# Decay sums by DMA from DRAM, in place of TensorE matmuls, in a hybrid state-space, attention and expert layer

## The chip, the cores and the metric

The kernel runs on one NeuronCore of a Trainium2 chip. Its engines are TensorE (PE, with its weight loads as PEld), VectorE (DVE), ScalarE (ACT), GpSimd (POOL) and SyncE (SP); SP, ACT and POOL issue DMAs. The metric is the device time of one execution in microseconds (us). L365 is line 365 of the kernel before.

## The reference: what is computed

One layer over 512 tokens of width 1024, in float32. After a norm and a projection, two branches run: a state-space branch (SSD) with 32 heads in 4 groups, in 4 chunks of 128 tokens, and windowed attention with 16 heads. They are gated, merged, projected and added to x. Then each token goes through 2 of 64 experts. The part that matters here:

```python
a_cum = jnp.cumsum(dt_c * a.reshape(G, J), axis=2)      # 32 heads, 4 chunks of 128 tokens
seg = a_cum[:, :, :, None] - a_cum[:, :, None, :]
decay = jnp.exp(jnp.where(causal, seg, -jnp.inf))
y_diag = jnp.einsum('bclsgj,bcsgjp->bclgjp', cb[..., None] * decay, xdt)
y_off = jnp.einsum('bclgn,bcgjpn->bclgjp', cm, prev) * jnp.exp(a_cum)[..., None]
```

For each head the kernel thus needs the running sums of all 512 tokens, one row of 512 numbers, on every partition, beside the same sums with the token on the partition.

## The kernel before, in words

The first half works with the channels or the tokens on the 128 partitions. proj() (L185) loads 1 MB of weights on SP's queue into one of two w buffers, splits it into a high part (ACT, L181) and a low part (DVE, every fifth time GpSimd, L182), and multiplies in three passes (L196 to L198) into the PSUM tag mm. The stages that call it (xbc_stage, z_stage, gate_stage, yssd0, yssd1) are written in the order of L639 to L673, with ssd_main(g) for the four groups among them. Behind them come the attention output and the output projection (L676 to L769), the router, and the experts (from L772), whose weights stream through two rings of buffers, ra and rb, on SP's queue; rb lies in memory that the first half gives back.

dt_stage (L210) makes the running sums: acum, with a token of a chunk on each partition and 4 x 32 columns (chunk, head). Four transposes turn a doubled copy of it, so that PSUM holds the 32 head rows twice; aT then holds the rows' high parts on partitions 0 to 31 and what is left on 32 to 63, with zeros below. sel holds two stacked identities.

ssd_main(g) makes the products of its group, and then four pairs of heads. decay(i, u) spreads head h's row over the partitions with one matmul (L365: sel's column h as the stationary operand, aT as the moving one) into the PSUM tag sb, which has two banks. ACT takes the exponential of half of it into E (L368), DVE takes the minimum with acum (L369) into M, and ACT takes four exponentials in M, one for each chunk (L374). heads(i) multiplies M with the masked products cbm, on DVE for u = 0 and on GpSimd for u = 1 (L386), runs the matmuls of the pair (L382, L390), and adds what belongs together (L392 to L395). A pair's decay is written one pair ahead of its heads (L397 to L401). cbm, E, M, btok and xx are v tiles, of which there are 10 buffers (L140); ssd_norm, the attention, the output projection and the router use the same tag.

The program order isn't the order on the engines. The tile framework plans each engine's order when the program is built (L1283), with its own estimate of every instruction's time; PE's matmuls of later stages so stand between those of ssd_main. Each engine then runs its list in order, and so does each DMA queue. The sb banks are used by ssd_norm, the attention's scores and the router as well. GpSimd issues the stores of gtd (L636), the gates, which SP loads again as c (L681, L682); ACT issues the loads of g2t (L702), a row of 512 numbers spread over 128 partitions from DRAM.

Of the kernel before, what the change touches and what calls it, by code (L numbers as in the profile page):

```python
# [7 lines left out]
F = mybir.dt.float32  # L8
R = mybir.dt.float32r
# [3 lines left out]
AF = mybir.ActivationFunctionType  # L13
OP = mybir.AluOpType
# [16 lines left out]
def tile_hybrid(ctx: ExitStack, tc: tile.TileContext, x, pos, cols, rows, g2d, wrd, wdtd, wcm, wqkv, wso, wao, wo,  # L31
                wgu, wdn, out):
    nc = tc.nc
    V, S, T, G = nc.vector, nc.scalar, nc.tensor, nc.gpsimd
# [4 lines left out]
    def ptile(tag, bufs=2, dt=F):  # L39
        return psum.tile([128, 512], dt, name=tag, tag=tag, bufs=bufs)  # L40

    p1 = ctx.enter_context(ExitStack())
    py, pg, pw, px, pb, pc, pz, pv = [p1.enter_context(tc.tile_pool(name=n, bufs=1, side="right"))
                                      for n in ("py", "pg", "pw", "px", "pb", "pc", "pz", "pv")]
# [4 lines left out]
    ident = cp.tile([128, 128], F, name="ident")  # L49
# [15 lines left out]
    mhalf, half = mh2[:, 0:1], mh2[:, 1:2]  # L65
    V.memset(mhalf, -0.5)
    V.memset(half, 0.5)
    sel = pb.tile([128, 32], R, name="sel")
    G.memset(sel.bitcast(F), 0.0)
    V.tensor_tensor(sel[0:64], ident[0:64, 0:32], ident[0:64, 32:64], op=OP.add)  # L70
    colt = pb.tile([128, 168], F, name="colt")
    S.dma_start(colt, cols)
    n1g, sng, dsk, n2g = colt[:, 0:8], colt[:, 8:24], colt[:, 24:40], colt[:, 160:168]
# [40 lines left out]
    dram = ctx.enter_context(tc.tile_pool(name="dram", bufs=1, space=bass.MemoryType.DRAM))  # L114
    h2d = dram.tile([512, 1024], F, name="h2d")
    tabd = dram.tile([128, 4 * NBK], I32, name="tabd")
    gwd = dram.tile([1024, 1], F, name="gwd")
    gtd = dram.tile([2, 8, 128, 512], F, name="gtd")

    def wslot(pool, tag, bufs, dt=F):  # L120
        return pool.tile([128, 2048], dt, name=tag, tag=tag, bufs=bufs)
# [8 lines left out]
    def tk(pool, tag, bufs, n, dt=F, name=None):  # L130
        return pool.tile([128, n], dt, name=name or tag, tag=tag, bufs=bufs)
# [5 lines left out]
    def a_(dt=F): return tk(pa, "a", 8, 512, dt)  # L137
    def w_(): return tk(pw, "w", 2, 2048, F)
    def g_(): return tk(pg, "g", 4, 1024, R)
    def v_(dt=F, n=512): return pv.tile([128, n], dt, name="v", tag="v", bufs=10, padded_shape=[128, 512])  # L140
    def c_(dt=F, n=512): return pc.tile([128, n], dt, name="c", tag="c", bufs=6, padded_shape=[128, 512])


# [2 lines left out]
    for t in range(4):  # L146
        xt = [x_(), x_()]
        for u in range(2):
            nc.sync.dma_start(xt[u], x[t * 128:(t + 1) * 128, u * 512:(u + 1) * 512])
        xs_.append(xt)  # L150
    wdt = v_(n=256)
    nc.sync.dma_start(wdt, wdtd)
    for t in range(4):
# [12 lines left out]
    for k in range(8):  # L166
        p = ptile(("tp", "sb", "y", "tp")[k // 2])
# [34 lines left out]
    dt = pb.tile([128, 128], F, name="dt")  # L202
    acum = pb.tile([128, 128], F, name="acum")
    dec = pb.tile([128, 128], F, name="dec")
    cd = pb.tile([128, 128], F, name="cd")
    nacum = pb.tile([128, 128], F, name="nacum")
    aT = pb.tile([128, 512], R, name="aT")
    G.memset(aT[64:128].bitcast(F), 0.0)

    def dt_stage():  # L210
        wd = g_()
        V.memset(wd.bitcast(F), 0.0)
        w3 = wd.rearrange("p (k c) -> p k c", k=8)
        r3 = wdt.rearrange("p (k c) -> p k c", k=8)
        S.activation(w3[:, :, 0:32], r3, AF.Copy)
        V.tensor_tensor(w3[:, :, 32:64], r3, w3[:, :, 0:32].bitcast(F), op=OP.subtract)
        p = ptile("mm")
        for k in range(8):
            T.matmul(p, w3[:, k, :], hh[k], start=(k == 0), stop=False)
            T.matmul(p, w3[:, k, :], hl[k], start=False, stop=(k == 7))  # L220
        dtT = v_()
        S.activation(dtT[0:64], p[0:64], AF.Copy)
        p = ptile("tp")
        for t in range(4):
            T.transpose(p[:, t * 64:(t + 1) * 64], dtT[0:64, t * 128:(t + 1) * 128], ident[0:64, 0:64])
        p3 = p[:, 0:256].rearrange("p (t u h) -> p t u h", t=4, u=2)
        xr = v_(n=128)
        x3 = xr.rearrange("p (t h) -> p t h", t=4)
        V.tensor_tensor(x3, p3[:, :, 0, :], dtb[:, None, :].to_broadcast([128, 4, 32]), op=OP.add)
        V.tensor_tensor(x3, x3, p3[:, :, 1, :], op=OP.add)  # L230

        e = v_(n=128)
        V.tensor_scalar(e, xr, -1.0, None, op0=OP.mult)
        V.tensor_tensor(e, e, xr, op=OP.min)
        S.activation(e, e, AF.Exp)
        s1 = v_(n=128)
        V.tensor_scalar(s1, e, 2.0, None, op0=OP.add)
        V.reciprocal(s1, s1)
        V.tensor_tensor(s1, s1, e, op=OP.mult)
        s2 = v_(n=128)  # L240
        V.tensor_tensor(s2, s1, s1, op=OP.mult)
        q = v_(n=128)
        V.tensor_scalar(q, s2, 1.0 / 17, 1.0 / 15, op0=OP.mult, op1=OP.add)
        for c in (13, 11, 9, 7, 5, 3, 1):
            V.tensor_tensor(q, q, s2, op=OP.mult)
            V.tensor_scalar(q, q, 1.0 / c, None, op0=OP.add)
        V.tensor_tensor(q, q, s1, op=OP.mult)
        V.tensor_scalar(xr, xr, 0.0, None, op0=OP.max)
        V.scalar_tensor_tensor(dt, q, 2.0, xr, op0=OP.mult, op1=OP.add)
        ea = v_(n=32)  # L250
        S.activation(ea, alog, AF.Exp)
        da = v_(n=128)
        V.scalar_tensor_tensor(da.rearrange("p (t h) -> p t h", t=4), dt.rearrange("p (t h) -> p t h", t=4), -1.0,
                               ea[:, None, :].to_broadcast([128, 4, 32]), op0=OP.mult, op1=OP.mult)
        pc = ptile("tp")
        T.matmul(pc[:, 0:128], tri, da, start=True, stop=True)
        T.matmul(pc[:, 128:256], ones, da, start=True, stop=True)
        V.tensor_copy(acum, pc[:, 0:128])
        V.tensor_scalar(nacum, acum, -1.0, None, op0=OP.mult)
        S.activation(cd, pc[:, 128:256], AF.Exp)  # L260
        V.tensor_tensor(dec, pc[:, 128:256], acum, op=OP.subtract)
        S.activation(dec, dec, AF.Exp)
        a2 = v_(n=256)
        a2v = a2.rearrange("p (t u h) -> p t u h", t=4, u=2)
        for u in range(2):
            V.tensor_copy(a2v[:, :, u, :], acum.rearrange("p (t h) -> p t h", t=4))
        pt = ptile("tp")
        for t in range(4):
            T.transpose(pt[0:64, t * 128:(t + 1) * 128], a2[:, t * 64:(t + 1) * 64], ident)
        S.activation(aT[0:32], pt[0:32], AF.Copy)  # L270
        hv = v_(R)
        S.activation(hv[32:64], pt[32:64], AF.Copy)
        V.tensor_tensor(aT[32:64], pt[32:64], hv[32:64].bitcast(F), op=OP.subtract)

    dt_stage()


# [44 lines left out]
    def ssd_main(g):  # L322
        BT, CT = bc[g, 0], bc[g, 1]
        p = ptile("tp")
# [6 lines left out]
        p = ptile("tp")  # L331
# [10 lines left out]
        for c in range(4):  # L342
            p = ptile("tp")
# [16 lines left out]
        def decay(i, u):  # L360
            h = 8 * g + 2 * i + u
            if u == 0:
                Es[i] = v_()
            pb_ = ptile("sb")
            T.matmul(pb_, sel[:, h:h + 1].to_broadcast([128, 128]), aT, start=True, stop=True)  # L365
            M = v_()
            us = slice(u * 64, (u + 1) * 64)
            S.activation(Es[i][us, 0:384], pb_[us, 128:512], AF.Exp)  # L368
            V.tensor_tensor(M.rearrange("p (c l) -> p c l", c=4), pb_.rearrange("p (c l) -> p c l", c=4),  # L369
                            acum.rearrange("p (c h) -> p c h", c=4)[:, :, h:h + 1].to_broadcast([128, 4, 128]),  # L370
                            op=OP.min)
            for c in range(4):
                s = slice(c * 128, (c + 1) * 128)
                S.activation(M[:, s], M[:, s], AF.Exp, bias=nacum[:, c * 32 + h:c * 32 + h + 1])  # L374
            return M


        def heads(i, Ms):
# [16 lines left out]
            G.tensor_tensor(y[:, 128:512], y[:, 128:512], E[:, 0:384], op=OP.add)  # L395

        both = lambda i: [decay(i, u) for u in range(2)]  # L397
        nxt = both(0)
        for i in range(4):
# [320 lines left out]
    for ct in range(4):  # L720
# [6 lines left out]
        pt = [ptile("tp"), ptile("tp")]  # L727
        for tp in range(2):
            p = ptile("mm")
            for ti in range(2):  # L730
                t = 2 * tp + ti
# [98 lines left out]
    for q in range(3):  # L830
        T.matmul(pk[:, q * 64 + 64:256], oneb, ob[:, None, q * 64:(q + 1) * 64].to_broadcast([128, 3 - q, 64]),
                 start=False, stop=False)
# [3 lines left out]
                    op=OP.mult)  # L836
# [450 lines left out]
```

## Time and profile before

| | |
|---|---|
| median of 3 runs | 1230.36 us (1229.38 to 1231.33) |
| the profiled execution | 1228.64 us |
| its span, first to last instruction | 1226.80 us |
| PE busy | 1136.3 us, 93% |
| DVE busy | 656.5 us, 54% |
| ACT busy | 388.6 us, 32% |
| POOL busy | 239.3 us, 20% |
| moved by DMA | 273.86 MB |

Busy is the time in which an engine has an instruction under way. PE's matmuls overlap, so a busy PE can still be waiting for its own pipeline. DMAs that GpSimd issues go through a queue that the profile calls software_dynamic; those of SP and ACT through hardware_dynamic queues. A wait is listed with the instruction that waited, the one that ended its wait, the sum, the number of times and the longest.

### The profile page before, as it was taken

The page shows a single profiled execution, that of the slowest core. Times are in us where ns is not written, and L with a number is a line of the kernel's source. Part 1 is how long each engine was busy: PE and PEld are TensorE (multiplying, and loading weights), DVE is VectorE, ACT ScalarE, POOL GpSimd, SP SyncE. Part 2 cuts the span into 40 slices and gives each one's busy share as a digit, 9 for nine tenths or more (in the row PEclk, how much of TensorE's full clock was granted, in tenths as well). Part 3 has the DMA queues.
Part 4 walks back from the last instruction along what each step waited for, and adds up shares of the span by engine and source line. Part 5 has one row for each costly group of instructions (what it writes and reads, how often), then busy time and mean ns, then how long its engine had stood idle before and what let it go on. Part 6 is the DMA issues. An engine that isn't in the chain of part 4 may idle for free.

```text
span 1226.8 us, 16583 instructions
## 1 busy us (share of the span) xinstructions
PE 1136.3 (93%) x6552; PEld 772.2 (63%) x6552; DVE 656.5 (54%) x1224; ACT 388.6 (32%) x796; POOL 239.3 (20%) x195
## 2 busy tenths in 40 slices
PE   6999999999999999999999959999897899999885
PEld 5777778877878988988778956443342434434321
DVE  5958584569536678877665464634422233331422
ACT  5456453464326455634432311110110011111000
POOL 3033431143024533330120241001001001000100
PEclk9999999999999999999999989999999899999999
DMA  4231213221221222222357257999999999999995
GB/s 157 98 118 38 100 61 129 94 79 54 83 104 35 70 104 87 87 69 69 137 168 300 110 235 305 419 420 420 420 419 421 420 415 398 387 420 419 421 419 221
DMA packets 43120, 273.86 MB, mean 223 GB/s; under 512 B 5024, under 2 KB 5664, under 8 KB 11808
## 3 DMA queue, kind: packets, MB, share of 16 engines
q1 hardware_dynamic: 39744, 263.34, 54.1%
q0 software_dynamic: 1712, 7.34, 1.6%
q10 hardware_dynamic: 1584, 2.10, 0.6%
q8 instruction: 52, 0.85, 0.3%
q14 instruction: 28, 0.23, 0.1%
HBM read 266.47 MB, written 6.29 MB: 222 GB/s over the span
## 4 chain that ended last, share of the span: by engine, by line
PE 77%; DVE 10%; DMA 8%; issue 2%; ACT 2%; POOL 1%; SPq 0%; DVEq 0%; ACTq 0%; POOLq 0%
PE mm L196 11%; PE mm L198 11%; PE mm L197 11%; PE mm L904 11%; PE y L925 5%; PE tp L884 5%; DMA rb<-in_wgu_dram 3%; PE tp L1003 3%; DVE acc L1005 2%; PE mm L481 2%; PE tp L1004 2%; PE mm L480 2%; DMA ra<-in_wdn_dram 2%; DMA rb<-in_wdn_dram 2%; PE mm L482 2%
## 5 line engine op out<-in xcount | busy, mean ns | idle before, releaser
L196 PE MATMUL mm<-h,g 128*128 128x512 f32 x448 | 180.7, 403 | 0.8 <-DVE c L309 0.5
L197 PE MATMUL mm<-h,g 128*128 128x512 f32 x448 | 179.8, 401 | 0.0
L198 PE MATMUL mm<-h,g 128*128 128x512 f32 x448 | 178.5, 399 | 0.8 <-POOL g L182 0.8
L904 PE MATMUL mm<-rb,st 128*32 128x512 f32 x712 | 145.6, 619 | 13.3 <-DMA rb<-in_wgu_dram 13.3
L181 ACT ACTIVATE g<-w 128x1024 fp32r<-128x1024 f32 x100 | 105.6, 1057 | 139.4 <-PE mm L197 99.0
L182 DVE TENSOR_TENSOR g<-w,g 128x1024 fp32r<-128x1024 f32 x78 | 98.7, 1265 | 72.9 <-ACT g L181 69.9
L1005 DVE TENSOR_TENSOR acc<-acc,tp 128x512 f32<-128x512 f32 x132 | 86.1, 684 | 37.2 <-PE tp L1004 37.0
L993 POOL TENSOR_SCALAR wk<-dr,vcol 128x512 fp32r<-128x512 int16 x17 | 26.6, 1565 | 383.8 <-PE tp L1004 347.9
L198 PEld LDWEIGHTS mm<-h,g 128*128 128x128 f32 x448 | 84.4, 188 | 22.2 <-POOL g L182 1.5
L196 PEld LDWEIGHTS mm<-h,g 128*128 128x128 f32 x448 | 84.5, 189 | 20.3 <-issue 1.2
L197 PEld LDWEIGHTS mm<-h,g 128*128 128x128 f32 x448 | 84.5, 189 | 19.8 <-issue 1.7
L182 POOL TENSOR_TENSOR g<-w,g 128x1024 fp32r<-128x1024 f32 x22 | 53.8, 2446 | 169.3 <-ACT g L181 138.5
L904 PEld LDWEIGHTS mm<-rb,st 128*32 128x32 f32 x712 | 30.9, 113 | 79.9 <-issue 55.8
L925 PE MATMUL y<-rb,n 128*32 128x512 f32 x384 | 72.0, 641 | 4.0 <-ACT n L916 3.3
L904 PE MATMUL mm<-ra,st 128*32 128x512 f32 x312 | 75.5, 597 | 0.0
L884 PEld LDWEIGHTS tp<-oh,hx 128*128 128x128 f32 x480 | 60.1, 191 | 23.6 <-issue 14.9
L931 DVE TENSOR_TENSOR yo<-y,yo 128x512 fp32r<-128x512 f32 x34 | 23.5, 691 | 92.3 <-ACT yo L930 92.3
L884 PE MATMUL tp<-oh,hx 128*128 128x256 f32 x480 | 66.7, 289 | 3.9 <-DVE m L956 3.6
L1003 PE MATMUL tp<-yo,wk 128*128 128x512 f32 x132 | 59.2, 465 | 11.1 <-DVE acc L1005 11.0
L1003 PEld LDWEIGHTS tp<-yo,wk 128*128 128x128 f32 x132 | 23.6, 187 | 69.6 <-DVE acc L1005 39.2
L909 ACT ACTIVATE n<-mm,gts 128x256 f32<-128x256 f32 x17 | 8.0, 473 | 180.6 <-PE mm L904 161.7
L910 DVE SCALAR_TENSOR_TENSOR n<-n,mm 128x256 f32<-128x256 f32 x17 | 7.1, 421 | 92.6 <-ACT n L909 92.6
(378 smaller groups left out, 2269.4 us busy)
## 6 DMA issues: line engine op xcount, KB each, us to landing
rb<-in_wgu_dram SPq DMA_DIRECT2D x89, 1024.0 KB, 15.1
rb<-in_wdn_dram SPq DMA_DIRECT2D x48, 1024.0 KB, 17.8
ra<-in_wgu_dram SPq DMA_DIRECT2D x39, 1024.0 KB, 12.5
w<-in_wcm_dram SPq DMA_DIRECT2D x27, 1024.0 KB, 4.9
ra<-in_wdn_dram SPq DMA_DIRECT2D x16, 1024.0 KB, 18.1
w<-in_wso_dram SPq DMA_DIRECT2D x8, 1024.0 KB, 4.9
w<-in_wqkv_dram SPq DMA_DIRECT2D x6, 1024.0 KB, 4.8
gtd<-c POOLq DMA_DIRECT2D x16, 256.0 KB, 2.5
```

Of the source, the lines that this page charges most:

```text
L181: S.activation(hi[:, :n], src, AF.Copy)
L182: (G if nsp[0] < 3 or nsp[0] % POOL_LO == 0 else V).tensor_tensor(lo[:, :n], src, hi[:, :n].bitcast(F), op=OP.subtract)
L196: T.matmul(p, hi[:, s], mh[k], start=(k == 0), stop=False)
L197: T.matmul(p, hi[:, s], ml[k], start=False, stop=False)
L198: T.matmul(p, lo[:, s], mh[k], start=False, stop=(k == 7))
L480: T.matmul(o, hh[k][:, ts], hi[:, s], start=(k == 0), stop=False)
L884: T.matmul(p[:, u * 256:(u + 1) * 256], hx[h][:, t, (k + u) * 128:(k + u + 1) * 128], oh[:, t], start=(h == 0 and t == 0), stop=(h == 1 an ...
L904: T.matmul(pg[e * 32:(e + 1) * 32], sts[u // 2][:, k, c:c + 32], wt[u, k // 4, e][:, (k % 4) * 512:(k % 4 + 1) * 512], start=(k == 0), sto ...
L925: T.matmul(py[n][e * 32:(e + 1) * 32], hT[:, f * 128 + e * 32:f * 128 + e * 32 + 32], wt[u, 2, e][:, ws], start=(f == 0), stop=(f == 1))
L993: G.tensor_scalar(wk, drow[0], vcol[:, b:b + 1], None, op0=OP.is_equal)
L1003: T.matmul(p, wk[:, t * 128:(t + 1) * 128], yhl[n][0], start=True, stop=False)
L1005: V.tensor_tensor(acc[t][:, ns], acc[t][:, ns], p, op=OP.add)
```

## The change

The 32 rows of running sums go to a DRAM tensor acd once. For each head, a DMA on GpSimd's queue reads its row from there 128 times, into a tile of the new tag rw, which has two buffers in SBUF. L368 and L369 read this tile instead of a PSUM bank. sel, the doubled copy a2, the split into high and low parts and the lower rows of aT go; the transposes take 32 columns each, and aT becomes a v tile. The v tag has 9 buffers instead of 10.

```diff
-    sel = pb.tile([128, 32], R, name="sel")
-    G.memset(sel.bitcast(F), 0.0)
-    V.tensor_tensor(sel[0:64], ident[0:64, 0:32], ident[0:64, 32:64], op=OP.add)
...
+    acd = dram.tile([32, 512], F, name="acd")
...
-    def v_(dt=F, n=512): return pv.tile([128, n], dt, name="v", tag="v", bufs=10, padded_shape=[128, 512])
+    def v_(dt=F, n=512): return pv.tile([128, n], dt, name="v", tag="v", bufs=9, padded_shape=[128, 512])
...
-    aT = pb.tile([128, 512], R, name="aT")
-    G.memset(aT[64:128].bitcast(F), 0.0)
...
-        a2 = v_(n=256)
-        a2v = a2.rearrange("p (t u h) -> p t u h", t=4, u=2)
-        for u in range(2):
-            V.tensor_copy(a2v[:, :, u, :], acum.rearrange("p (t h) -> p t h", t=4))
+
         pt = ptile("tp")
         for t in range(4):
-            T.transpose(pt[0:64, t * 128:(t + 1) * 128], a2[:, t * 64:(t + 1) * 64], ident)
+            T.transpose(pt[0:32, t * 128:(t + 1) * 128], acum[:, t * 32:(t + 1) * 32], ident)
+        aT = v_()
         S.activation(aT[0:32], pt[0:32], AF.Copy)
-        hv = v_(R)
-        S.activation(hv[32:64], pt[32:64], AF.Copy)
-        V.tensor_tensor(aT[32:64], pt[32:64], hv[32:64].bitcast(F), op=OP.subtract)
+        nc.sync.dma_start(acd, aT[0:32])
...
-            pb_ = ptile("sb")
-            T.matmul(pb_, sel[:, h:h + 1].to_broadcast([128, 128]), aT, start=True, stop=True)
+            pb_ = pv.tile([128, 512], F, name="rw", tag="rw", bufs=2)
+            G.dma_start(pb_, acd[h:h + 1].to_broadcast([128, 512]))
```

## Rows read from the trace of the kernel before

**Rows 1.** Busy time by stretch: PE, PEld, DVE, ACT, POOL, PEclk, DMA share, GB/s

```profile
45.00:660.00 615.00, 610.18 (x3415) 499.88 (x3415) 412.90 (x703) 291.73 (x608) 177.12 (x137) 1.00 0.26 91
104.40:113.10 8.70, 8.70 (x52) 6.62 (x51) 7.90 (x14) 6.50 (x16) 3.17 (x3) 1.00 0.36 123
720.00:1150.00 430.00, 378.25 (x2236) 170.65 (x2235) 163.11 (x355) 51.80 (x99) 34.40 (x26) 0.96 0.99 408
```

**Rows 2.** PE's waits, 45 to 660 (us, times, longest): first, last of eight

```profile
PE sb L414 <- DVE v L412: 1.5, 1, 1.5
PE mm L196 <- DVE c L685: 0.2, 1, 0.2
```

**Rows 3.** SP's queue at the first half's end: a wait, the timeline

```profile
SPq L779 <- PE mm L738: 38.9, 2, 38.4
719.85 1.87 SPq L779 DMA_DIRECT2D rb<-in_wdn_dram  x4
```

**Rows 4.** PE timeline: L365 and what follows it, three of its places

```profile
64.68 0.71 PE L365 MATMUL sb<-aT,sel 128*128 128x512 f32 x2
65.23 0.39 PE L196 MATMUL mm<-h,g 128*128 128x512 f32 x1
...
153.08 0.39 PE L365 MATMUL sb<-aT,sel 128*128 128x512 f32 x1
153.32 0.40 PE L197 MATMUL mm<-h,g 128*128 128x512 f32 x1
...
387.14 0.73 PE L365 MATMUL sb<-aT,sel 128*128 128x512 f32 x2
387.71 0.28 PE L480 MATMUL mm<-g,h 128*128 128x256 f32 x1
```

**Rows 5.** Timelines of ACT, DVE, POOL, PE: one pair of group 3

```profile
382.45 1.00 ACT L368 ACTIVATE v<-sb 64x384 f32<-64x384 f32 x2 [1.17 <-PE sb L365]
...
383.04 1.29 DVE L369 TENSOR_TENSOR v<-sb,acum 128x512 f32<-128x512 f32 x2 [0.33 <-ACT v L368]
...
386.30 1.28 POOL L386 TENSOR_TENSOR v<-v 128x512 f32<-128x512 f32 x1 [2.50 <-ACT v L374]
...
390.51 1.09 PE L390 MATMUL y<-v,x 128*64 128x128 f32 x16
```

**Rows 6.** PE timeline, L390: one pair and the last, groups 0, 2, 3

```profile
104.40 1.09 PE L390 MATMUL y<-v,x 128*64 128x128 f32 x16
...
119.68 1.09 PE L390 MATMUL y<-v,x 128*64 128x128 f32 x16
...
276.71 1.09 PE L390 MATMUL y<-v,x 128*64 128x128 f32 x16
...
290.22 1.09 PE L390 MATMUL y<-v,x 128*64 128x128 f32 x16
...
380.84 1.09 PE L390 MATMUL y<-v,x 128*64 128x128 f32 x14
...
396.60 1.09 PE L390 MATMUL y<-v,x 128*64 128x128 f32 x16
```

**Rows 7.** Sources L636, then L702; issues of c<-gtd: time to landing

```profile
L636 POOL DMA_DIRECT2D gtd<-c x16: 539/572/817, 66.3 to 615.4; - x16
...
DMA to landing us min/median/max: 2.3/2.5/7.2
...
DMA to landing us min/median/max: 4.0/4.7/5.4
...
c<-gtd SPq DMA_DIRECT2D x16, 256.0 KB, 3.4
```

**Rows 8.** Sources L369, L386, L412 on DVE: ns min/median/max

```profile
L369 DVE TENSOR_TENSOR v<-sb,acum x32: 674/682/692, 87.6 to 388.9; 128x512 f32<-128x512 f32 x32
...
L386 DVE TENSOR_TENSOR v<-v x16: 673/692/1643, 90.1 to 390.3; 128x512 f32<-128x512 f32 x16
...
L412 DVE TENSOR_SCALAR v<-ident,v x16: 275/285/2405, 169.3 to 486.3; 128x128 f32<-128x128 f32 x16
```

## The prediction, made before the result was known

> **What bounds the kernel now.** I read the page's slices first, to split the run. Up to about 660 us the projections, the state-space stage and the attention run; behind that come the output projection, the router and the experts. Then the busy time by stretch [rows 1]. From 45 to 660 PE is busy for 610.2 of 615.0 us at a granted clock of 1.00, with the DMA engines at 0.26 of their time. From 720 to 1150 this turns round: the DMA engines are at 0.99 and move 408 GB/s, and PE has 378 of 430 us. So the first half is PE's and the second the expert weights'. Next, who waits for whom: in 615 us PE waits in eight places, from 1.5 us down to 0.2, 4.7 us in all [rows 2]. Nothing but its own work holds PE there. Last, what joins the halves. The SP queue that issues the expert weights waits 38.4 us for the output projection's matmuls to give their memory back, and goes on at 719.85 [rows 3]. The weight stream behind that point keeps its length, so what PE saves ahead of 719.85 should come off the end one for one, and what it loses should be added.
>
> **The change part by part.** *32 matmuls go (L365).* Matmuls overlap, so the duration in a row (0.39 us) is not the price; the step from one start to the next is. Between two projection matmuls L365 takes 153.32 - 153.08 = 0.24 us; a pair between other work takes 65.23 - 64.68 = 0.55 us at the first place and 387.71 - 387.14 = 0.57 us at the last [rows 4]. The 32 stand in 26 places, 20 single and 6 in pairs; their steps add up to 5.3 + 3.4 = 8.7 us. Part of the dearer steps is the change of operand kind, which may stay with the neighbours: 32 x 0.235 = 7.5 us is the floor. I take the middle, 8.1 us.
>
> *What prepared them goes* (sel, the memsets, two copies, one ACT copy and one subtraction in dt_stage), and four transposes get narrower. No PE wait in [rows 2] names any of them, and matmuls of xbc_stage(0) cover them: nothing. Were that cover gone, it would be a gain, of under 1 us each. The store of the 32 rows is one more DMA on SP's queue ahead of weight loads; these already wait for their buffers, and PE's list shows no wait for a weight: nothing. If one were late, L181's split and PE would be next.
>
> *32 loads come, of 256 KB each, on GpSimd's queue.* Their issue costs GpSimd what gtd's does, 0.57 us [rows 7], 18 us in all; GpSimd is busy for 177 of 615 us [rows 1], so that is no bound by itself. As bandwidth 8.4 MB are nothing beside a share of 0.26. The path is the question: a load must land before L368 and L369 can read. No row shows this load. Below, the nearest is a 256 KB store on the same queue, median 2.5 us; c<-gtd, a load of that size, has 3.4; g2t (L702), the same form, one 2 KB row spread over 128 partitions, but on ACT's queue, has 4.0 to 5.4 and a middle of 4.7; the longest of any is 7.2 [rows 7]. I take 4.7, for its form.
>
> Where is that late? The two slots replace the two PSUM banks: a load for the next pair may go once L369 has read the slot. The tightest group is the last, with (396.60 - 380.84) / 3 = 5.25 us a pair, against 7.6 in group 0 and 6.8 in group 2 [rows 6] (group 1 is taken as group 2). In group 3 a pair's last L369 ends at 383.04 + 1.29 = 384.33 [rows 5], and the next pair's matmuls are done at 387.71 [rows 4], 3.4 us later. A load of 3.4 us thus changes nothing; one of 4.7 is 1.3 late at each of three hand-overs, 3.9 in all. Against it stands the slack behind the chain: L386 on GpSimd ends at 386.30 + 1.28 = 387.58 and PE takes the product at 390.51 [rows 5], 2.9 us later. So 1.0 us of stall at 4.7; 3 x 2.0 - 2.9 = 3.1 at 5.4; none at 3.4 or 2.5. The other groups have 1.5 to 2.4 us more in each pair and stall nowhere up to 5.4. I take +1.0, bounds 0 and +3.1.
>
> GpSimd runs in order. Behind an issue that waits for its slot stand L386 and L395 of the pair before, and the low halves of every fifth weight split (L182), for which PE waits next. But the slot comes free at L369, before L374 has even finished what L386 needs, and GpSimd idles 2.50 us there [rows 5]: nothing, within the bounds above.
>
> *L369 and L368 read SBUF in place of PSUM.* L369 now has both operands in SBUF, as L386 on DVE has. L386's median is the same (692 against 682 ns), its longest 1643 against 692 [rows 8]. From 104.4 to 113.1 DVE is busy for 7.90 of 8.70 us [rows 1], so in group 0 it has little to spare. Bounds: nothing, and 8 x 0.96 = 7.7 us if all eight of group 0 took the longest. I take +0.5, since the median says that most don't. The Trainium skill (SBUF — State Buffer, section "SBUF: two separate sides") gives a reason: a VectorE instruction with two SBUF inputs and a GpSimd instruction that reads SBUF shut each other out for a whole instruction. The trace agrees, with the 1643 ns beside 692.
>
> *One v tile less.* By the code a pair holds cbm, two E and four M, with btok and xx early in a group; ssd_norm's yn use what is left. Its wait at L414, 1.5 us [rows 2], is the nearest row: nothing, or 4 x 1.5 = 6.0 if each group gets one. I take nothing, since two slots still alternate.
>
> The sum: -8.1 + 1.0 + 0.5 = -6.6 us. The profiled execution took 1228.64 us, 1226.80 of span and 1.84 around it, so 1222.0 by its own time; the median of the runs is 1.7 us above it, which gives 1230.4 - 6.6 = **1223.8 us**. The likeliest case's own range is from the full 8.7 saved to 7.5 saved with 3.1 of stall: 1221.7 to 1226.
>
> **The rivals.** *DVE takes the place of PE in group 0.* For: the 0.8 us that it has left there. Against: PE waits for DVE in hardly any place. At the long end, -8.1 + 1.0 + 7.7 = +0.6: 1231, no change; half of it gives 1227.
>
> *Loads land late (slower).* One mechanism at one place, the hand-over of the two slots: at landing L group 3 loses 3 x (L - 3.4) - 2.9, groups 1 and 2 each 3 x (L - 4.9) - 2.9, group 0 3 x (L - 5.8) - 2.9. At 6.3 us that is 5.8 + 1.3 + 1.3 = 8.4, and the gain is gone; at 7.2, the longest of rows 7, it is 8.5 + 4.0 + 4.0 + 1.3 = 17.8, so -8.1 + 17.8 + 0.5 = +10.2: 1240.6. For: 128 reads of one row, and a planner that fixes every engine's order when the program is built, so that a late head stops PE although other work is there. Against: the median of gtd is 2.5.
>
> *DVE holds up the descriptors.* Issues on GpSimd's queue took 539 to 817 ns [rows 7], so something sometimes stretches them. If each of the 16 L412 (285 ns at the median, [rows 8]) held one load that PE waits for, that would be 4.6 us: 1228.4, no change. The Trainium skill (SBUF — State Buffer, same section) speaks against this change: DMAs from GpSimd's queue can't be described while VectorE runs copies in its fast two-port mode, so such loads belong on SP's or ACT's queue. The trace leaves it open: few such copies stand in these stages, and no row shows a load that waited for one.
>
> *One v tile less costs its 6.0*: 1229.8, no change.
>
> *More than the sum.* The sb banks are left to ssd_norm and the attention, and the planner may fill better: the 4.7 us of waits [rows 2] could go too, 1219.
>
> **How the numbers follow.** Likeliest 0.50; DVE 0.18; late loads 0.17; descriptors 0.05; the v tile 0.03; more than the sum 0.07. About 0.2%, 2.5 us, is what a measurement of this kernel can tell from no change. Faster: 0.50 + 0.07 = 0.57. Same: 0.18 + 0.05 + 0.03 = 0.26. Slower: 0.17. For 8 in 10 the range takes in the DVE case and the start of the late loads, and half of the better case: 1220.5 to 1233.
>
> **What would show it.** The saving: 128 x 512 matmuls of L365 gone and PE still at over 98% from 45 us to the end of the attention; the SP wait behind the output projection ends 6 to 7 us sooner, near 713. The stall: the loads' landing, under 5 us, and PE waits for M or L386 of about 1 us in group 3 alone. DVE: L369's median near 0.69 and its longest over 1 us. I'm wrong if PE waits several us at L390 or for L182's low halves, if the loads land after 6 us, or if PE saves its 8 us and the experts' stream still starts at the old time.

## The result, and the profile after

The change makes the kernel slower by 0.8%: 1239.97 us (median of 4 runs, 1238.88 to 1241.85) against 1230.41 (4 runs, 1229.38 to 1231.33), ratio 1.008, 95% interval 1.0062 to 1.0097. The forecast was 1223.8 with a range to 1233.0. The profiled execution took 1239.95 us with a span of 1238.0, 11.2 more than before. Lines have moved: L365, L368, L369, L374, L386, L390 and L392 to L395 of before are now L357 (the load), L360, L361, L366, L378, L382 and L384 to L387; L374 now is L382 of before.

Where the time went is read first from SP's queue, at the point where it goes on behind the output projection [rows 3]:

```profile
725.81 1.87 SPq L771 DMA_DIRECT2D rb<-in_wdn_dram  x4
```

Before, this row stood at 719.85. So the first half is 6.0 us *longer*, though the 32 matmuls are gone, and from here to the end of the span it takes 512.2 us in place of 506.95, 5.2 longer. Both have to be explained. Below, "first half" is this row's start and "second half" the rest of the span.

Busy time by stretch, columns as in [rows 1], the three stretches of before and then five of 5 us:

```profile
45.00:660.00 615.00, 601.00 (x3358) 492.95 (x3358) 417.48 (x696) 292.29 (x607) 198.92 (x169) 0.99 0.31 103
104.40:113.10 8.70, 6.82 (x48) 5.40 (x47) 8.70 (x12) 5.96 (x15) 7.16 (x6) 1.00 0.59 199
720.00:1150.00 430.00, 378.77 (x2283) 174.89 (x2283) 163.59 (x357) 52.22 (x102) 35.81 (x28) 0.96 0.97 401
...
270.00:275.00 5.00, 4.12 (x33) 3.30 (x31) 2.53 (x5) 1.30 (x4) 1.55 (x2) 1.00 0.93 274
275.00:280.00 5.00, 1.70 (x14) 1.54 (x16) 4.08 (x7) 4.95 (x14) 2.81 (x4) 0.75 0.26 80
280.00:285.00 5.00, 5.00 (x25) 4.17 (x22) 4.57 (x7) 1.48 (x4) 5.00 (x5) 0.57 0.17 52
430.00:435.00 5.00, 2.03 (x14) 1.42 (x12) 3.94 (x10) 4.38 (x8) 2.31 (x3) 0.95 0.46 193
435.00:440.00 5.00, 5.00 (x18) 3.95 (x17) 1.71 (x4) 0.50 (x2) 2.87 (x2) 0.71 0.00 0
```

From 45 to 660 PE now idles for 14.0 us (615.0 - 601.0) where it idled for 4.8 [rows 1], and in two places the idle is followed by a stretch at the lower clock: the mean grant is 0.57 in 280 to 285, so nearly all of it at 1.2 instead of 2.4 GHz, and 0.71 in 435 to 440. Summed as 5 x (1 - clock) over slices of 5 us this is up to 5.1 us more; before, the clock was 1.00 throughout. In 104.4 to 113.1 DVE has no time left at all, 8.70 of 8.70, and PE has 6.82 where it had 8.70.

PE's waits from 45 to 680 us (us, times, longest), to be held against [rows 2], whose longest was 1.5:

```profile
PE y L374 <- DVE v L384: 5.0, 3, 1.9
PE tp L536 <- DVE c L499: 3.0, 1, 3.0
PE y L382 <- ACT c L300: 2.8, 1, 2.8
```

The first and third are the heads of ssd_main. The second is the q and k stage, which the change doesn't touch; it is taken up again under the order. In their places: 1.88 us at 112.08 (L374, group 0, where DVE is full), 1.39 and 2.79 at 275.51 and 279.24 (L374 and L382, end of group 2), 1.72 at 395.54 (L374, end of group 3) and 2.97 at 434.59 (L536).

The loads themselves, source L357 (durations of the issue in ns, what GpSimd waited for ahead of it, who waited for the load), beside [rows 7]:

```profile
L357 POOL DMA_DIRECT2D rw<-acd x32: 536/547/812, 59.9 to 389.5; - x32
its engine sat idle before it (us, times) until:
  DMA acd<-v: 17.1, 1
  DVE v L361: 10.4, 6
  ACT v L366: 10.2, 6
...
who waited for it (us, times):
  ACT v L360: 15.8, 10
  DVE v L361: 12.5, 9
...
DMA to landing us min/median/max: 3.3/3.6/7.8
```

Half of the loads land within 3.6 us, *sooner* than the 4.7 that were taken; yet ACT and DVE wait 28 us for them. How that reaches PE is seen at the end of group 2. GpSimd, ACT, DVE and PE there, each from its own timeline:

```profile
268.29 0.58 POOL L357 DMA_DIRECT2D rw<-acd  x1 [1.76 <-ACT v L366]
271.10 0.54 POOL L357 DMA_DIRECT2D rw<-acd  x1 [2.23 <-DVE v L361]
```

```profile
273.70 0.52 ACT L360 ACTIVATE v<-rw 64x384 f32<-64x384 f32 x1 [4.08 <-DMA rw<-acd]
274.13 1.26 ACT L366 ACTIVATE v<-v,nacum 128x128 f32<-128x128 f32 x4
275.30 1.04 ACT L179 ACTIVATE g<-w 128x1024 fp32r<-128x1024 f32 x1
```

```profile
269.88 0.69 DVE L361 TENSOR_TENSOR v<-rw,acum 128x512 f32<-128x512 f32 x1
...
273.69 0.69 DVE L361 TENSOR_TENSOR v<-rw,acum 128x512 f32<-128x512 f32 x1 [2.47 <-DMA rw<-acd]
...
276.38 1.45 DVE L180 TENSOR_TENSOR g<-w,g 128x1024 fp32r<-128x1024 f32 x1 [0.92 <-ACT g L179]
277.75 0.68 DVE L361 TENSOR_TENSOR v<-rw,acum 128x512 f32<-128x512 f32 x1
278.35 0.73 DVE L386 SCALAR_TENSOR_TENSOR x<-x,colt,y 128x512 f32<-128x512 f32 x1
```

```profile
275.51 0.94 PE L374 MATMUL y<-b,x 128*128 128x128 f32 x6 [1.39 <-DVE v L384]
279.24 1.97 PE L382 MATMUL y<-v,x 128*64 128x128 f32 x16 [2.79 <-ACT c L300]
```

The issue at 268.29 waits for its slot, which L361 leaves only at 267.76, and its load is long, 5.3 us to 273.6, with the DMA engines at 0.93 of their time in 270 to 275. It is the load of the *next* pair, which PE doesn't need yet. But ACT runs its list in order, and L360 of the next pair stands ahead of L366 of this pair's second head, whose minimum has been ready since 270.6 (269.88 + 0.69). So this pair stops too, for 4.1 us, and with it the high part of a weight split (L179), DVE's low part behind that (L180), and L386, which reads the pair before out of its bank of the PSUM tag y and ends at 279.08 (278.35 + 0.73). By the code L382 writes into that bank, so it can't start before; the profile names L300 of ACT, which ended at 279.20 (278.62 + 0.58) and stood behind the same late load in ACT's list. Either way the load holds PE. Then PE runs at half clock: L382's 16 matmuls take 1.97 us, before 1.09 [rows 6].

At the end of group 3 two things meet: a load that lands late, and the minimum behind it, which takes 2.58 us where the median is 0.69. PE's 1.72 us at 395.54 are for L384, which stands behind this minimum in DVE's list.

```profile
392.43 2.58 DVE L361 TENSOR_TENSOR v<-rw,acum 128x512 f32<-128x512 f32 x1 [1.29 <-DMA rw<-acd]
```

Together this accounts for the first half, as an estimate: 9.2 us more of idle (14.0 - 4.8) and up to 5.1 us of clock, against the 8.1 that the matmuls were taken to save, make up to 6.2; measured are 6.0.

### The profile page after: what moved, and what is told of

It is laid out like the page before. It is cut to its first block, busy times and chain, and to the rows that moved or that the text cites. A ratio compares the mean times of both kernels' runs of the same rounds, so it can differ in the third digit from the quotient of the medians.

```text
span 1238.0 us, 16589 instructions
## 1 busy us (share of the span) xinstructions
PE 1133.7 (92%) x6520; PEld 769.6 (62%) x6520; DVE 663.6 (54%) x1220; ACT 391.2 (32%) x797; POOL 260.6 (21%) x225
## 4 chain that ended last, share of the span: by engine, by line
PE 71%; DMA 13%; DVE 9%; ACT 3%; issue 2%; POOL 1%; SPq 0%; DVEq 0%; POOLq 0%; ACTq 0%
PE mm L194 11%; PE mm L196 11%; PE mm L195 11%; PE mm L896 9%; DMA rb<-in_wgu_dram 6%; PE y L917 5%; PE tp L876 4%; DMA ra<-in_wdn_dram 3%; PE tp L995 2%; DMA rw<-acd 2%; DVE acc L997 2%; DMA rb<-in_wdn_dram 2%; PE tp L996 1%; DVE v L361 1%; PE mm L473 1%
## 5 line engine op out<-in xcount | busy, mean ns | idle before, releaser
L179 ACT ACTIVATE g<-w 128x1024 fp32r<-128x1024 f32 x100 | 105.6, 1057 | 141.6 <-PE mm L195 109.3
L180 DVE TENSOR_TENSOR g<-w,g 128x1024 fp32r<-128x1024 f32 x78 | 100.8, 1292 | 57.2 <-ACT g L179 55.7
L180 POOL TENSOR_TENSOR g<-w,g 128x1024 fp32r<-128x1024 f32 x22 | 53.9, 2450 | 174.0 <-ACT g L179 113.3
L896 PE MATMUL mm<-ra,st 128*32 128x512 f32 x312 | 72.3, 596 | 0.0
```

Of the source, the lines that this page charges most:

```text
L179: S.activation(hi[:, :n], src, AF.Copy)
L180: (G if nsp[0] < 3 or nsp[0] % POOL_LO == 0 else V).tensor_tensor(lo[:, :n], src, hi[:, :n].bitcast(F), op=OP.subtract)
L896: T.matmul(pg[e * 32:(e + 1) * 32], sts[u // 2][:, k, c:c + 32], wt[u, k // 4, e][:, (k % 4) * 512:(k % 4 + 1) * 512], start=(k == 0), sto ...
```

## The experiments

18 kernels ran. Of most, the table gives first and second half (profiled execution), the median, and the ratio to the kernel before on the same chip with its 95% interval. The halves come from one execution each: "profile" is how far that one lay from the median, up to 4.5 us, so differences of 2 to 3 us between halves can be chance. Kernels with the same letter under "order" run the second half in the same order on every engine, but for at most 19 of PE's 2539 matmuls; "-" is an order of its own.

| run | first half | second half | order | profile | median | ratio |
|---|---|---|---|---|---|---|
| before | 719.85 | 506.95 | A | -1.8 | 1230.4 | |
| the change | 725.81 | 512.2 | B | 0.0 | 1240.0 | 1.008 (1.0062 to 1.0097) |
| v9_alone | 719.10 | 506.7 | A | -1.7 | 1229.3 | 1.0006 (0.9997 to 1.0015) |
| into_M | 722.64 | 514.3 | - | +0.2 | 1238.5 | 1.0074 (1.006 to 1.0087) |
| act_queue | 715.47 | 506.6 | C | -3.1 | 1227.0 | 0.9984 (0.9973 to 0.9996) |
| sp_queue | 718.93 | 508.2 | C | +0.8 | 1228.2 | 0.9988 (0.9978 to 0.9997) |
| act_groups_2_3 | 723.41 | 506.1 | C | -0.2 | 1231.5 | 1.0015 (1.0001 to 1.003) |
| act_groups_0_1 | 723.11 | 509.4 | B | -2.2 | 1236.5 | 1.0058 (1.0042 to 1.0073) |
| act_into_M | 720.25 | 512.0 | F | -0.1 | 1234.2 | 1.004 (1.0025 to 1.0054) |
| unread_loads | 731.19 | 515.6 | - | +4.5 | 1244.2 | 1.0111 (1.0095 to 1.0128) |
| unread_4slots | 725.52 | 508.9 | A | 0.0 | 1236.2 | 1.0058 (1.0042 to 1.0073) |
| same_work_new_order | 720.60 | 513.5 | D | +2.7 | 1233.1 | 1.0024 (1.0011 to 1.0038) |
| act_queue_new_order | 727.11 | 510.9 | - | +3.3 | 1236.5 | 1.006 (1.0046 to 1.0073) |
| pool_new_order | 730.25 | 511.6 | E | +1.3 | 1242.7 | 1.0106 (1.0089 to 1.0123) |
| before_order_3 | 721.41 | 509.5 | D | -0.2 | 1233.0 | 1.0021 (1.0012 to 1.0031) |
| pool_order_3 | 729.30 | 509.8 | F | -1.4 | 1242.7 | 1.0102 (1.0081 to 1.0123) |
| act_order_3 | 726.47 | 506.5 | E | -0.1 | 1234.9 | 1.0042 (1.0027 to 1.0057) |
| matmuls_back_unread | 735.82 | 514.7 | - | +2.6 | 1249.9 | 1.0167 (1.0151 to 1.0183) |
| act_products_on_DVE | 714.96 | 511.4 | - | -0.3 | 1228.4 | 0.9998 (0.9986 to 1.0011) |

**The loads, their slots, their queue, the v tile.** From the changed kernel:

```diff
# four_loads
+            if (i, u) == (0, 0):
+                Es["row"] = pv.tile([128, 512], F, name="rw", tag="rw", bufs=2)
+                G.dma_start(Es["row"], acd[h:h + 1].to_broadcast([128, 512]))
+            pb_ = Es["row"]
# into_M (v with 11 buffers, no rw)
+            G.dma_start(M, acd[h:h + 1].to_broadcast([128, 512]))
+            pb_ = M
# act_queue
-            G.dma_start(pb_, acd[h:h + 1].to_broadcast([128, 512]))
+            S.dma_start(pb_, acd[h:h + 1].to_broadcast([128, 512]))
# v9_alone: the kernel before, v with bufs=9
```

> Leaves out 28 of the 32 loads: each group loads the row of its first head once and all eight heads read it, so the decays of the other heads are computed from a wrong row. Everything else is as in the changed kernel, L361 with two SBUF inputs included. If late loads cost the time: the 8.1 us of matmuls saved come through, 1220 to 1226 us, PE above 98% from 45 us to the end of the attention, no fall of the granted clock there. If L361 and L360 reading SBUF beside GpSimd cost it: 1232 to 1240 us, L361 still up to 1.7 us. If the v tile costs it: 1234 to 1240.

It took 1296.6 us, but only the first half can be read: with the wrong decays tokens go to other experts, and matmuls of the extra blocks (from L1186 on) run at the end, which the kernel before has not. Its first half ends at 721.96, with 11.1 us of idle on PE from 45 to 660: 3.8 sooner than the changed kernel, 2.1 later than before. So the loads are not all of it, against the theory of late loads; the longest wait, 3.7 us, is in a norm's diagonal (L408 behind L406).

> The loads go straight into M, and L361 takes the minimum in place; the two slots of rw become v tiles (11). If the hand-over of the two slots is what makes the loads late: they are issued earlier, and the time is 1222 to 1231 us. If the landing time itself, or GpSimd's order, makes them late: 1236 to 1241. If L361 beside GpSimd costs the time: 1236 to 1241, with no wait for loads in the list.

1238.5: with no hand-over of two slots the first half is 3.2 us shorter than the changed kernel's, and the second half 2.1 us longer. Landing is 3.3/4.4/7.1 us here, and ACT still waits 14.7 us for loads.

> The loads are issued by ScalarE instead of GpSimd, the two slots stay. If GpSimd's order (issues behind L378 and L387) makes them late: 1228 to 1234 us, and landing under 3 us after the issue. If two slots and the landing make them late: 1237 to 1243, since ScalarE adds 32 issues of about 0.05 to 0.6 us to its own exponentials. If L361 costs the time: 1238 to 1242.

1227.0, the first half 10.3 us sooner, in a profile that lay 3.1 us below the median. The same view of L357:

```profile
L357 ACTq DMA_DIRECT2D rw<-acd x32: 326/326/461, 60.9 to 384.4; - x32
...
  ACT v L360: 6.7, 8
  DVE v L361: 4.5, 7
...
DMA to landing us min/median/max: 3.0/3.3/5.1
```

The landing is only 0.3 us shorter at the median, but an issue stands right behind the work that frees its slot, and ACT and DVE wait 11 us for loads in place of 28.

> The kernel before with one v buffer less, nothing else. If the v tile is free, as predicted: 1229.5 to 1231.5 us. If it costs its share (6.0 us was the bound): 1233 to 1237, with waits of PE for DVE in the norm of a group or in the q and k stage (2 to 3 us).

Nothing: this term was right.

**Is it the queue?** In unread_loads the kernel before keeps its matmuls and issues the loads beside them, for nobody; unread_4slots takes a quarter of each row and so has four buffers.

```diff
# unread_loads (v with 9 buffers, the store of aT to acd as in the change)
+            rw = pv.tile([128, 512], F, name="rw", tag="rw", bufs=1)
+            G.dma_start(rw, acd[h:h + 1].to_broadcast([128, 512]))
             pb_ = ptile("sb")
# unread_4slots
+            rw = pv.tile([128, 128], F, name="rw", tag="rw", bufs=4)
+            G.dma_start(rw, acd[h:h + 1, 0:128].to_broadcast([128, 128]))
# act_groups_2_3 (act_groups_0_1 with g < 2); act_into_M is into_M with S.dma_start; sp_queue has nc.sync.dma_start
+            (S if g >= 2 else G).dma_start(pb_, acd[h:h + 1].to_broadcast([128, 512]))
```

> The kernel before with its 32 matmuls kept, and the 32 loads issued on GpSimd's queue beside them, into one buffer that nobody reads (9 v buffers, to make room). Nobody waits for the loads, so only their issue on GpSimd and their traffic are left. If the wait for the loads is what cost the time in the changed kernel: 1228 to 1232 us, as before. If the 18 us of issues on GpSimd, or the traffic, cost it: 1234 to 1240.

1244.2: 14 us more than before for loads that nobody reads. GpSimd's waits from 45 to 410 us, and PE's from 45 to 680:

```profile
POOL rw L367 <- DMA rw<-acd: 64.2, 24, 5.1
```

```profile
PE tp L354 <- POOL v L352: 4.3, 2, 2.7
```

With one buffer every issue waits for the load before it, 64 us in all, and GpSimd's products behind it come late; PE waits for one of them (L352, xx). The single buffer makes this harder than the change, where GpSimd waits 27 us ahead of its issues, the first one aside.

> As the run with unread loads, but the 32 loads take only the first 128 numbers of a row, so four buffers fit in the place of one: as many issues on GpSimd's queue, a quarter of the bytes, and hardly an issue that waits for its buffer. The planned order of the second half is that of the kernel before. If issues that wait for a buffer, and so hold up GpSimd's products, made the run with unread loads slow: 1228 to 1232 us, and GpSimd's waits for the loads near nothing instead of 64 us. If the issue itself, or a load on that queue beside VectorE, costs it: 1236 or more.

1236.2, with only 3.5 us of such waits on GpSimd. Half of the 14 us goes, half stays: the first half still ends 5.7 us later than before, at an unchanged order of the second. PE idles 3.3 us more (8.1 against 4.8); the rest is in no wait that I found, and part of it can be chance. So even issues that hardly wait cost time here; whether by the 0.55 us that each takes of GpSimd or by the order that was planned around them, this run can't say.

> The changed kernel with the loads of groups 2 and 3 issued by ScalarE, those of groups 0 and 1 still by GpSimd. The changed kernel lost most of its time at the end of group 2 (275 us) and behind group 3. If that is GpSimd's queue in these groups: the first half ends within 2 us of the kernel with all loads on ScalarE (715.5), and the whole takes 1226 to 1230 us. If groups 0 and 1 carry as much of it: 1231 to 1236. The planned order of the second half is nearly that of the kernel with all loads on ScalarE: if the order sets the length of the second half, it is 506 to 507.5 us from the first wait for the output projection's memory to the end, not 512.

> The reverse: groups 0 and 1 by ScalarE, 2 and 3 by GpSimd. If GpSimd's queue costs in groups 2 and 3: the first half ends at 721 to 726, and the whole takes 1234 to 1240 us; if groups 0 and 1 carry as much: 1229 to 1233. The planned order of the second half is that of the changed kernel: if the order sets its length, it is 511 to 513 us again.

Not as expected in the first half: both end near 723, 7.9 and 7.6 us behind act_queue, so the parts don't add up to the 10.3 us that ScalarE's queue gained. The second halves took 506.1 in the order of act_queue and 509.4 in that of the changed kernel, which lies between its 512.2 and the 507 of before.

> The changed kernel with the loads on SP's queue, which runs no arithmetic, but issues the weights in the same order. If it was GpSimd's products and issues standing in each other's way: as with ScalarE, 1224 to 1230 us, second half 506 to 507.5. If ScalarE's advantage is that its issues stand right behind the exponentials that free a slot: SP holds the weight loads behind an issue that waits, and it takes 1230 to 1240.

1228.2, as with ScalarE. SP does no arithmetic, so no product waits behind an issue there; this speaks for GpSimd's mix of issues and products as the cost. Nor is it the traffic, since the same 32 rows move here and on ScalarE's queue. The landing is 3.0/3.2/6.4 us.

> Loads by ScalarE, straight into M, 11 v buffers: no hand-over of two slots and nothing of GpSimd's order. If both the slots and GpSimd's queue held the chain: 1219 to 1225 us, with waits for the loads in the heads near nothing. If the slots are of no account, as the run with the loads into M on GpSimd's queue makes likely: 1225 to 1229, as with ScalarE alone; if the planner's order is a lottery of several us, anything from 1222 to 1234, with a second half that differs from 507 us.

Worse than act_queue in both halves, 4.8 and 5.4 us: without the hand-over nothing is won. The order is another too, so what costs them isn't separated.

**Is it the order?** The table of sines (rope_tab) is made elsewhere: for the new order behind the first ssd_main, for the third ahead of kv_stage. Each move was made in the kernel before, with GpSimd's loads and with ScalarE's.

```diff
-    rope_tab()
...
     ssd_main(0)
+    rope_tab()
```

> The kernel before; only the small table of sines is made behind the first ssd_main instead of ahead of all stages. The work is the same, and PE's planned order differs by some 27 instructions in each half. If the order that the planner happens to find is worth several us by itself: more than 2 us from 1229.5 in either direction, above all in the second half (507 us). If not: 1228.5 to 1231.

> The kernel with all loads on ScalarE's queue, with the same move of the table: 52 instead of 16 instructions of PE stand elsewhere in the second half. If the planned order sets the second half, it leaves 506.6 us by 2 us or more, and the whole is 1228 to 1236; if the loads on ScalarE's queue are better whatever the order: 1225 to 1229.

> The changed kernel (loads on GpSimd's queue) with the table of sines made behind the first ssd_main, the same move that cost the kernel before 0.24% and the kernel with loads on ScalarE 0.8%. If GpSimd's queue costs time whatever the order: 1238 to 1250 us, above the 1236.5 of the same program with ScalarE's queue. If the loss of the changed kernel was the order it happened to get: it can fall to 1228 to 1236.

> The kernel before with the table made ahead of the k and v stage, a third order of the same work (93 instructions of PE elsewhere in the first half, 25 in the second). If the order is worth several us in the second half alone: first half within 1.5 us of 719.9, second half anywhere from 506 to 514, the whole 1229 to 1236 us.

> The changed kernel with the same move. GpSimd's queue systematic: first half above that of the next run by 4 us or more, the whole 1236 to 1246 us. Order alone: no such difference, 1226 to 1240.

> Loads on ScalarE's queue with the same move. If ScalarE's queue keeps part of the 32 matmuls' time whatever the order: first half below 720, the whole 1224 to 1233 us. If its gain was the order it happened to get: first half 720 to 727, the whole 1230 to 1238.

In the kernel before, the move leaves the first half nearly alone (719.85, 720.60, 721.41); by the medians it costs 3.6 and 2.9 us, though the work is the same. With GpSimd's loads the first half ends 6.0, 9.7 and 7.9 us later than before with the table in the same place, and the whole takes 9.6, 9.0 and 9.7 us longer (medians, each first set against the kernel before on the same chip). With ScalarE's the first half ends 4.4 us sooner, then 6.5 and 5.1 later, and the whole is 1.9 us shorter, then 3.4 and 1.9 longer. So GpSimd's loss is there in all three places, and ScalarE's gain in one.

Not all of the first half's loss is the queue's, though. In the changed kernel PE's list has a transpose of the q and k stage (L536) right behind those of L515, and waits there for DVE:

```profile
430.58 1.03 PE L515 MATMUL tp<-ident,c 128*64 128x128 f32 x8
434.59 0.66 PE L536 MATMUL tp<-ident,c 128*128 128x128 f32 x2 [2.97 <-DVE c L499]
```

This wait of 3.0 us, with up to 1.7 us of lower clock behind it, stands in six kernels: the change, act_groups_0_1, pool_new_order, pool_order_3, matmuls_back_unread, and act_order_3, whose loads are on ScalarE's queue. In all the others 24 projection matmuls stand between the two, and there is no such wait. So up to 4.7 us of these first halves are a planned order in a stage that the change leaves alone. Without them the three losses with GpSimd's loads would be about 1.3, 5.0 and 3.2 us, an estimate.

The second half's 5.2 us stay open. Kernels of one order differ there as much: 512.2 and 509.4 (B), 513.5 and 509.5 (D), 511.6 and 506.5 (E). So neither the order nor the change is shown to be the cause, and part can be chance.

Part of where it is lost shows at the end. The chain that ended last, in the changed kernel, in same_work_new_order, and in act_groups_0_1:

```profile
1206.81 6.58 PE mm L896 x26
...
1215.82 5.95 PE y L917 x32
```

```profile
1205.37 6.62 PE mm L904 x26
...
1214.43 5.96 PE y L925 x32
```

```profile
1213.96 3.62 PE y L917 x20
```

In the first two the last expert's matmuls take 6.6 us for 26 where most earlier ones of the chain take 3.6: the granted clock is 0.59 to 0.72 from 1205 to 1220 in the changed kernel, and in the kernel before it is 1.00 there. act_groups_0_1 has the changed kernel's order, but ends, like before, with 20 matmuls in 3.62 us.

The moved table is no neutral load for the changed kernels. In act_queue_new_order DVE makes it at 109.87 (2.80 us), in the part of group 0 that is full, and PE waits 3.5 us for the convolution behind it (L275). The kernel before hides the same table.

**Is PE still the bound, and why is DVE slower?**

```diff
# matmuls_back_unread, from the changed kernel
+            T.matmul(ptile("sb"), hh[0][:, 0:128], hh[1], start=True, stop=True)
             M = v_()
# act_products_on_DVE, from act_queue
-                (G if u else V).tensor_tensor(Ms[u], Ms[u], cbm, op=OP.mult)
+                V.tensor_tensor(Ms[u], Ms[u], cbm, op=OP.mult)
```

> The changed kernel, loads on GpSimd's queue and read as there, with 32 matmuls of the old size put back beside them, whose products nobody reads. If PE were still what bounds the first half, they cost their 6 to 8 us again: the first half ends at 731 to 734, the whole is 1245 to 1249 us. If the heads' chain (loads, DVE, ACT, GpSimd) now sets the pace and PE only waits less, the first half ends within 2 us of 725.8 or earlier, and the waits of PE and the stretches at half clock shrink by what the matmuls take.

The first half ends at 735.82, 10.0 us after the changed kernel's. PE still pays for the matmuls, and the stalls stand beside them undiminished (14.9 us of idle from 45 to 660).

> The kernel with loads on ScalarE's queue, with all 32 products M times cbm on VectorE instead of half of them on GpSimd. If VectorE's longer minima (1.07 us instead of 0.68 on average) come from GpSimd working in SBUF at the same time: the minima fall to below 0.8 us on average, 12 us of busy time come back on VectorE for the 11 us that the 16 products cost it, and the first half stays within 3 us of the same kernel's in its three orders (715 to 727). If they come from the loads' writes into SBUF: the minima stay at 1 us, VectorE is 11 us fuller, and the first half ends at 727 or later.

The minimum from 80 to 415 us (busy us, mean ns, idle before), act_queue and then this run:

```profile
L361 DVE TENSOR_TENSOR v<-rw,acum 128x512 f32<-128x512 f32 x32 | 33.7, 1069 | 7.1 <-DMA rw<-acd 4.5 <-POOL x L387 2.3
```

```profile
L378 DVE TENSOR_TENSOR v<-v 128x512 f32<-128x512 f32 x32 | 28.7, 903 | 5.7 <-ACT v L366 5.6
L361 DVE TENSOR_TENSOR v<-rw,acum 128x512 f32<-128x512 f32 x32 | 25.8, 816 | 3.8 <-DMA rw<-acd 3.7
```

With GpSimd's 16 products moved to DVE, the minimum falls from 1069 to 816 ns, a little above the 0.8 that was expected, though the loads are the same. Of its stretch over the 683 ns of before that is 253 of 386 ns, so most of it is GpSimd, as far as a run with another order can show. The first half is the shortest of all, 714.96; the second, under yet another order, takes it back. act_queue and sp_queue are the only versions whose interval lies below that of before, by 0.1 to 0.2%, and act_queue's with the table in one place of three.

## Why the prediction was wrong

**PE's saving, -8.1.** Not contradicted. Putting 32 matmuls back costs 10.0 us of the first half, under an order that moved much else and in a profile 2.6 us above its median.

**The loads' stall, +1.0 (0 to +3.1).** This is the step that failed. Not by the landing: 3.6 us at the median where 4.7 was taken. It failed in two sentences around it. One let a late load cost only the pair that reads it, set off against 2.9 us of slack, and so had no stall outside group 3 up to a landing of 5.4 us; in the trace, at the end of group 2, a load of 5.3 us for the *next* pair stands ahead of this pair's exponentials in ACT's list and stops both, and a weight split behind them. The other said of an issue that waits in GpSimd's queue "nothing, within the bounds above"; GpSimd waited 27 us at its issues, and loads on its queue that nobody reads cost 6.7 and 14.3 us by themselves. It also had no term for the clock, which fell behind the long waits. Measured: at the end of group 2 alone PE waits 4.2 us (1.39 + 2.79) and loses up to 3.4 to the clock behind it, where the sum had 1.0 in all. With the matmuls put back, the first half is 16.0 us longer than before (735.82 - 719.85), where the sum had 1.0 + 0.5; up to 4.7 of this is L536's wait, for which no term stood either.

**DVE's second SBUF input, +0.5 (0 to 7.7).** Right in kind, mis-sized. L361 takes 988 ns at the mean in the changed kernel and 683 before, 31.1 against 21.2 us for 32: 9.9 us more on DVE. The median of 693 ns hides that, and the estimate went by such a median (L386's, 692). DVE then has 8.70 of 8.70 us in group 0, and PE waits there (L374 for L384, 1.88 us at 112.08), as it does behind the 2.58 us of group 3. What this costs of the end is not separated from the loads' part. The Trainium skill (SBUF — State Buffer, section "SBUF: two separate sides") says that a VectorE instruction with two SBUF inputs and a GpSimd instruction that reads SBUF take turns; act_products_on_DVE agrees, 1069 to 816 ns.

**The v tile, nothing.** Right: 1.0006. **The preparation and the store, nothing.** Not tried alone; the store lands in 1.6 us.

**One for one to the end.** It didn't come out: of the 11.2 us by which the span grew, 6.0 are the first half and 5.2 the second, which took 506.1 to 515.6 us over these kernels and 507.0 to 513.5 with the very same work. Its cause stays open. With the second half unchanged, the forecast would still have had the wrong sign.

**The rivals.** The slower one, loads late at the hand-over, was given 0.17 and came closest: its place is right, its price (a landing of 6.3 us or more) is not; the lateness is in when loads are issued and in what waits behind them. That its 1240.6, for a landing of 7.2 us, lies near the measured time is luck. The descriptors' rival finds little: the landing is 3.6 us on GpSimd's queue, 3.3 on ScalarE's and 3.2 on SP's, so moving the loads off GpSimd helped, but hardly for that reason.

**Left open**: how the first half's loss divides between GpSimd's waits at issues, the 0.55 us of each, and the order that is planned around them; why both mixed runs end near 723; and what lengthens the second half.

## What to carry to other kernels

When one engine is full and others run ordered lists beside it, price a load by what stands behind it in the list of the engine that waits, not by its landing alone, and keep DMA issues that must wait for a buffer off a queue whose engine also computes for the critical one. Where a planner fixes the order, run the kernel before under two or three orders of the same work first: here that alone moved it by 0.2%, and the changed kernel must be held against each, by the medians and not by one profile. Check what a saved instruction hid: the kernel before hid 2.8 us of extra VectorE work, and a changed one had PE wait 3.5 us behind it.

## What the runs showed of the hardware

A load of one 2 KB row onto 128 partitions took 3.2 to 3.6 us at the median on GpSimd's, ScalarE's and SP's queues (4.4 in into_M); an issue took 0.33 us on ScalarE and 0.55 us on GpSimd. PE's waits of 2.8 and 3.0 us were followed by 5 us at a mean granted clock of 0.57 and 0.71, so that 16 small matmuls took 1.97 us in place of 1.09: these idles of TensorE cost more than their own time. A VectorE minimum that took 683 ns at the mean with one input in PSUM took 988 with both in SBUF beside GpSimd's work, and 2.58 us at the longest.
